# The first half of an encoder layer rebuilt: token-major inputs by chunks, 14 Strassen units, recurrence beside query/key, attention beside branch A

## The chip, the cores and the metric

One core of a Trainium2 chip runs one program. Its engines work side by side, each through its own list of instructions in order: PE (matmuls; PEld is the load of its stationary operand), DVE (vector), ACT (scalar), POOL (GpSimd) and SP, whose only work here is to issue transfers. Matmuls read SBUF and write PSUM, which has 8 banks of 128 x 512 fp32 here. The metric is the device time of one execution in microseconds (us); lower is better.

## The reference

One layer over 1024 tokens of width 1024: a gated linear recurrence (branch A), banded attention (branch B), their gated sum, a feed-forward block, and a gated embedding. Cut to what matters:

```
h = rmsnorm(x, norm_mix_g)
z = h @ w_in            # 5632 columns
qa, fa, ia, ga, qb, kb, vb, gate_a, gate_b = split(z)      # 7 x 512, 2 x 1024
oa = hgrn2_mixer(qa, fa, ia, ga, ...)    # 4 heads of 128: a recurrence over chunks with a decay per key
ob = band_attention(qb, kb, vb, ...)     # 8 heads of 64: each 64-token chunk sees itself and the 8 before
merged = sigmoid(gate_a) * (oa @ w_branch_a) + sigmoid(gate_b) * (ob @ w_branch_b)
x = x + merged @ w_out
h2 = rmsnorm(x, norm_ffn_g)
x = x + (silu(h2 @ w_ffn_gate) * (h2 @ w_ffn_up)) @ w_ffn_down
h3 = rmsnorm(x, norm_ple_g)
x = x + sigmoid(h3 @ w_ple_gate) * (p @ w_ple_proj)
```

## The kernel before, in words

Everything is fp32. The large products split each operand into a high part in a shortened fp32 form and the rest (`hi`, `lo`; names `wh`/`wl`, `whi`/`wlo` for weights, pairs of slots `s` for activations) and take three matmuls for one: high by high, high by low, low by high. ACT casts the high part, DVE or POOL subtracts to get the rest. Activations are kept feature-major, 8 tiles of 128 features x 1024 tokens, in 32 "slots" `s`; products go feature-major (`feature`: 512 tokens move past 128 features of weights) or token-major (`token`: 128 tokens are stationary, 256 or 512 feature columns of weights move).

In order of the program:

- `first_norm` loads x in 8 chunks of 512 KB, scales and splits each into `self.u`, and multiplies every chunk into four banks, which become q and f of head 0. The division by the norm is done when a bank is evicted (`self.r` by token, `self.rb` as rows), so products need not wait for it.
- `hgrn_in(0)`, the rest of head 0: the recurrence's i and g, token-major, 256 columns. `gate_sums` meanwhile makes the sums of activations that a Strassen product wants.
- `gate_units`: 7 units. One unit (`strassen`) makes 256 features of the two branch gates with 7 block products of 12 matmuls each where a plain product would take 8. `first_weights` makes a unit's operands from its raw weights (`gate_load`, two buffers of the pool `raw`), `quad_item` makes sums of weights that the output and down projections use much later, and the sigmoid of a gate is stored to DRAM.
- The recurrence: `hgrn_mix(h)` is woven with `hgrn_in(h + 1)` by `weave`, which compares the shares that two streams have done of a planned total; the fourth with `attn_v`, the values of attention. A head goes through 7 levels (m = 1 to 64): 8 small fp32 matmuls of kt by q on PE, then on DVE the products of q and of kt by the decay, which the next level's matmuls read, then a masked copy. Then 8 chunk steps, each of which reads `state` on PE and updates it on DVE.
- `attention`: 32 steps (4 pairs of heads x 8 token blocks), each with scores, row maximum, exponential, normalising, transposes, product by values. Filler from `feed` stands between: `attn_in`, the query/key products (token-major, 256 columns), then two plain gate chunks.
- `branches`: both branches' products times their gates; then `out_proj`, in `passes` of Strassen products, and the feed-forward block and the rest, which the change leaves alone.

The order on each engine is the order of the code (`order` ties each instruction of PE, SP and the ones given by `self.V`, `self.A`, `self.G` to the one before), and a tile's pool decides when a buffer comes free. All transfers but one small one are issued on SP, in order, and one that waits holds up those behind it.

## Time and profile before

| | |
|---|---|
| time of 3 runs | 1638.03 us median (1637.19 to 1640.42) |
| the profiled execution | 1640.24 us, of which the span from first to last instruction is 1638.5 us |
| granted clock of PE, mean | 0.991 |
| HBM read, written | 147.05 MB, 55.84 MB |
| transfers' share of the 16 DMA engines' span (queue q1) | 35.2% |

[...] The slices of the span show how evenly PE works and what clock it was granted:

```profile
PE   7999999999999999999898999999999999999998
DVE  8866666756649888665988788888888866536653
```

Each digit is the busy share of a fortieth of the span (41 us) in tenths. PE is at nine tenths or more but at the start and near the middle; DVE is busiest where attention runs (slices 12 to 16).

### The profile page before, as it was taken

Reading aid. Unit: us, or ns where it says so; the run is one execution under the profiler, and the core shown is the slowest. Engines: PE = TensorE matmul, PEld = TensorE weight load, DVE = VectorE, ACT = ScalarE, POOL = GpSimd, SP = SyncE. Lnnn points to the kernel's source line nnn. Section 1 sums busy time; section 2 is a strip of 40 time slices with the busy share of each in tenths; the row PEclk is TensorE's granted clock in tenths of the full one; section 3 lists DMA queues with packets and bytes.
Section 4 is the critical chain, followed back from the end, with each engine's and each line's share of the span. In section 5 each row is a group of like instructions: output and inputs, shape, how many; then the busy total and the mean of one; then the engine's idle time right before and its main releaser. Section 6 shows DMA issues by size and latency. Waiting matters only on the chain.

```text
span 1638.5 us, 22553 instructions
## 1 busy us (share of the span) xinstructions
PE 1590.3 (97%) x8656; PEld 1348.1 (82%) x8656; DVE 1191.1 (73%) x1838; ACT 618.3 (38%) x1080; POOL 702.1 (43%) x408
## 2 busy tenths in 40 slices
PE   7999999999999999999898999999999999999998
PEld 5877779899899999888686788888888888888887
DVE  8866666756649888665988788888888866536653
ACT  5523322122037777610365422222222234436321
POOL 2233342221143332114422587777666765546420
PEclk9999999999999999999999999999999999999999
DMA  5045550201020011178434323233222268555521
GB/s 186 27 134 193 202 204 16 102 27 52 27 76 16 29 43 45 47 301 291 174 129 180 128 97 110 97 109 117 97 97 97 79 248 305 208 195 185 194 77 52
DMA packets 70524, 204.36 MB, mean 125 GB/s; under 512 B 7952, under 2 KB 8720, under 8 KB 68496
## 3 DMA queue, kind: packets, MB, share of 16 engines
q1 hardware_dynamic: 70272, 202.90, 35.2%
q8 instruction: 68, 1.11, 0.3%
q14 instruction: 40, 0.33, 0.1%
q10 hardware_dynamic: 144, 0.02, 0.0%
HBM read 147.05 MB, written 55.84 MB: 124 GB/s over the span
## 4 chain that ended last, share of the span: by engine, by line
PE 44%; DVE 6%; DMA 1%; ACT 1%; issue 1%; POOL 0%; SPq 0%; DVEq 0%; ACTq 0%
PE pm L81 44%; DVE s L52 5%; DMA wr<-in_sg 1%; DVE wl L124 1%; ACT s L52 1%; DMA wr<-in_su 0%; DMA wr<-d 0%; DVE q L52 0%; ACT whi L52 0%; DVE pl L52 0%; DVE wr L52 0%; ACT wh L121 0%; POOL s L854 0%; SPq L76 0%; ACT q L52 0%
## 5 line engine op out<-in xcount | busy, mean ns | idle before, releaser
L81 PE MATMUL pm<-s,wh 128*128 128x512 f32 (+1 forms) x1688 | 527.6, 394 | 14.7 <-DVE s L52 9.1
L81 PE MATMUL pm<-s,whi 128*128 128x512 f32 x1568 | 490.3, 394 | 9.5 <-DVE s L52 5.0
L124 POOL TENSOR_TENSOR wl<-wr,wh 128x1024 fp32r<-128x1024 f32 (+2 forms) x100 | 250.0, 2506 | 367.0 <-ACT wh L121 356.0
L81 PEld LDWEIGHTS pm<-s,wh 128*128 128x128 f32 x1688 | 317.9, 190 | 82.7 <-DVE s L52 11.6
L81 PEld LDWEIGHTS pm<-s,whi 128*128 128x128 f32 x1568 | 295.2, 188 | 77.5 <-issue 3.1
L81 PE MATMUL pm<-s,wl 128*128 128x512 f32 (+1 forms) x844 | 330.6, 392 | 0.0
L81 PE MATMUL pm<-s,wlo 128*128 128x512 f32 x784 | 308.3, 393 | 0.3 <-DVE wlo L52 0.3
L52 DVE TENSOR_TENSOR s<-s,s 128x512 f32<-128x512 f32 (+3 forms) x202 | 252.6, 1277 | 74.2 <-ACT s L52 39.4
L81 PE MATMUL pm<-wh,s 128*128 128x256 f32 (+1 forms) x1152 | 252.1, 304 | 0.1
L121 ACT CAST wh<-wr 128x1024 fp32r<-128x1024 f32 (+2 forms) x106 | 106.3, 1005 | 286.5 <-PE pm L81 141.9
L52 POOL TENSOR_TENSOR wlo<-wr,whi 128x512 fp32r<-128x512 f32 x74 | 139.7, 1894 | 136.1 <-ACT whi L52 120.1
L81 PEld LDWEIGHTS pm<-wh,s 128*128 128x128 f32 x1152 | 191.4, 192 | 5.5 <-DVE s L52 0.3
L81 PEld LDWEIGHTS pm<-s,wl 128*128 128x128 f32 x844 | 160.7, 190 | 33.3 <-POOL wl L124 0.3
L81 PEld LDWEIGHTS pm<-s,wlo 128*128 128x128 f32 x784 | 147.8, 189 | 34.3 <-DVE wlo L52 0.7
L81 PE MATMUL pm<-wl,s 128*128 128x256 f32 (+1 forms) x576 | 170.5, 296 | 0.0
L52 DVE TENSOR_TENSOR t<-pm,t 128x512 f32<-128x512 f32 x143 | 98.1, 686 | 76.4 <-PE pm L81 71.2
L52 POOL TENSOR_TENSOR s<-s,t 128x512 f32<-128x512 f32 x44 | 75.4, 1713 | 90.0 <-ACT t L52 90.0
L81 PEld LDWEIGHTS pm<-wl,s 128*128 128x128 f32 x576 | 111.0, 193 | 2.1
L52 DVE TENSOR_TENSOR s<-pm,s 128x512 f32<-128x512 f32 x101 | 65.3, 683 | 60.6 <-PE pm L81 60.6
L52 ACT CAST whi<-q 128x512 fp32r<-128x512 f32 (+1 forms) x63 | 47.8, 758 | 155.2 <-DVE q L52 133.0
L81 PE MATMUL pm<-s,s 128*128 128x64 f32 (+4 forms) x776 | 99.2, 269 | 3.1 <-DVE s L52 2.9
L52 ACT CAST whi<-wr 128x512 fp32r<-128x512 f32 x90 | 67.2, 757 | 86.1 <-DVE wr L52 49.7
(141 smaller groups left out, 1954.3 us busy)
## 6 DMA issues: line engine op xcount, KB each, us to landing
s<-d SPq DMA_DIRECT2D x65, 512.0 KB, 5.4
d<-s SPq DMA_DIRECT2D x87, 256.0 KB, 2.7
d<-dq SPq DMA_DIRECT2D x60, 256.0 KB, 2.3
wr<-d SPq DMA_DIRECT2D x28, 512.0 KB, 3.6
dq<-in_wq SPq DMA_DIRECT2D x11, 1024.0 KB, 7.7
wr<-in_sg SPq DMA_DIRECT2D x22, 512.0 KB, 3.9
wr<-in_su SPq DMA_DIRECT2D x22, 512.0 KB, 4.2
d<-t SPq DMA_DIRECT2D x34, 256.0 KB, 2.8
```

The source lines that it names most:

```text
L52: return lambda *a, **k: self.trunk.order(op(*a, **k), self.key)
L81: return self.order(self.nc.tensor.matmul(*a, **k))
L121: self.nc.scalar.copy(hi[:, c], raw[:, c])
L124: rest.tensor_tensor(lo[:, c], raw[:, c], f32(hi[:, c]), ALU.subtract)
```

## The change

Everything up to the output projection is put in a new order; the feed-forward block and what follows stay.

- **First products.** Attention's values v (all 512 columns, 8 banks) are multiplied chunk by chunk as x arrives, the recurrence's i likewise in `second_rows`; both go to DRAM (`vd`, `id`) and are read back by head.
- **28 chunks in 14 units.** q, f, g of the recurrence and both branch gates (`CHUNKS`) are all made by Strassen units; q, f, g go to DRAM too and come back by `head_load`. A unit's raw weights are loaded alternately into the pool and into slots.
- **Recurrence.** The heads run one after the other (`heads`) with the query/key products as their filler (`attn_in`, now 512 columns, two token blocks at a time; scaled rows are stored to DRAM twice over, in pieces of 64, and loaded block by block). Some work moves from DVE to ACT: kt, the sums of squares, the scaling before the transposes.
- **Attention.** Keys of both heads of a pair lie side by side; the scores' sign is turned so that the minimum is taken; normalising moves from ACT and DVE to POOL; the transposes of both heads are copied four blocks at a time. The filler is what is left of query/key, then branch A's product (`branch_a`).
- **Branches and output projection.** Only branch B's products stay in `branches`; x is reloaded in two lots of four; the output projection's passes begin with the halves that are ready first (`OUT`).

```diff
-GATES = 7
+GATES = 14
+CHUNKS = [(n, h) for h in range(4) for n in "qf"] + [("g", h) for h in range(4)] + [(n, c) for n in "ab" for c in range(8)]
...
-        outs = [self.mm() for _ in range(4)]
+        outs = [self.mm() for _ in range(8)]
         xs = []
-        start = [self.unit() for _ in range(2)]
-        ws = [(hi, lo) for hi, lo, _, _ in start]
+        unit = self.unit()
         for k in range(KC):
             x = self.slot()
             sc = self.cols[:, C_MIX + k:C_MIX + k + 1]
+            if k and k % 2 == 0:
+                unit = self.unit()
+                self.unit_piece(unit, 0, D)
...
+            if k < KC - 1:
+                for b in range(8):
+                    self.token_step(outs[b], unit, k, b)
...
+        self.weights(0, ahead=2)
+        for b in range(8):
+            self.token_step(outs[b], unit, KC - 1, b)
+            if b == 0:
+                self.A.copy(piece(0), outs[0])
+            if b == 2:
+                self.norm_sums()
+        self.rows_out(outs, piece, 1)
+        self.A.activation(piece(0), piece(0), AF.Copy, scale=self.r[:, 0:1])
+        self.keep_rows(self.vd, got)
+
+    def token_step(self, ps, unit, k, b):
+        hi, lo = unit[:2]
+        c = slice(k % 2 * HALF, k % 2 * HALF + HALF)
+        ah, al = [t[:, b * P:b * P + P] for t in self.u[k]]
+        self.mul(ps, ah, hi[:, c], start=k == 0, stop=False)
+        self.mul(ps, ah, lo[:, c], start=False, stop=False)
+        self.mul(ps, al, hi[:, c], start=False, stop=k == KC - 1)
...
+    def second_rows(self):
+
+        outs = [self.mm() for _ in range(8)]
+        sums = self.gate_sums()
+        first = None
         for k in range(KC):
-            for i in (0, 2, 1, 3):
-                ah, al, bh, bl = pairs[i][k]
-                self.mul(outs[i], ah, bh, start=k == 0, stop=False)
-                self.mul(outs[i], ah, bl, start=False, stop=False)
-                self.mul(outs[i], al, bh, start=False, stop=k == KC - 1)
-        return outs
-
+            if k % 2 == 0:
+                (unit,) = self.weights(1, ahead=2)
+            for b in range(8):
+                self.token_step(outs[b], unit, k, b)
+            next(sums, None)
+            if k == 2:
+                first = self.gate_first()
+            if k > 3:
+                next(first, None)
...
-            raw = self.rp.tile([P, D], F32, tag="raw", name=f"wr{self.n}")
+            raw = self.slot() if len(self.sorder) % 2 else self.rp.tile([P, D], F32, tag="raw", name=f"wr{self.n}")
...
+                if kind == "g":
+                    s = self.stmp()
+                    A.activation(s, t, AF.Sigmoid)
+                    G.tensor_tensor(t, t, s, ALU.mult)
+                elif kind != "q":
+                    A.activation(t, t, AF.Sigmoid)
+                if kind == "f":
+                    G.tensor_scalar(t, t, self.lb1[:, i:i + 1], self.lb[:, i:i + 1], ALU.mult, ALU.add)
...
             def side():
-                more, item = iter(()), iter(())
+                more = iter(())
                 if n + 1 < GATES:
                     self.gate_load()
                     more = self.first_weights()
                 else:
-                    then()
+                    then(0)
                 flush()
-                if n:
-                    item = self.quad_item(1, 0)
-                    next(item)
-                yield
+                next(more, None)
+                for _ in range(2 if n else 0):
+                    next(item, None)
                 yield
                 next(more, None)
+                for _ in range(2 if n else 0):
+                    next(item, None)
+                yield
                 next(more, None)
...
+    def head_load(self, h):
+        q, f, v, g = self.hg[h] = [self.slot() for _ in range(4)]
+        self.load(f, self.gd[CHUNKS.index(("f", h))])
+        self.load(q, self.gd[CHUNKS.index(("q", h))])
+        self.rows_load(v, self.id, h)
+        self.load(g, self.gd[CHUNKS.index(("g", h))])
...
-        self.V.tensor_scalar(kt, f, -1.0, 1.0, ALU.mult, ALU.add)
+        nc.scalar.activation(kt, f, AF.Copy, scale=-1.0, bias=1.0)
...
-            yield 430 if m == 1 else 1560 if m < 32 else 1400 if m == 32 else 2000
+            yield 430 if m == 1 else 2400 if m < 32 else 1400 if m == 32 else 2000
...
-            yield 650
+            yield 450
...
+                for a in range(4):
+                    sl = slice(a * P, a * P + P)
+                    nc.scalar.activation(sq[:, sl], po[:, sl], AF.Square, accum_out=ss[:, a:a + 1])
...
+    def heads(self):
+        yield 10000
+        for h in range(4):
+            more = iter(())
+            if h < 3:
+                more = self.near(h + 1)
+            for i, ns in enumerate(self.hgrn_mix(h)):
+                yield ns
+                if i == 0 or i > 9:
+                    next(more, None)
...
+            to = self.qd[g, b] = self.spill()
+            for i in range(2):
+                self.store(
+                    to[:, :].rearrange("p (a two d) -> p a two d", two=2, d=64)[:, :, i, :], t[:, :].rearrange("p (a d) -> p a d", d=64))
+
+        for g in range(2):
+            ws = []
+            for two in range(0, 8, 2):
+                outs = [self.mm() for _ in range(2)]
+                for k in range(KC):
+                    if two == 0 and k % 2 == 0:
+                        ws += self.weights(1, ahead=3 - k // 2)
+                    for b in range(2):
+                        self.token_step(outs[b], ws[k // 2], k, two + b)
...
+        engine.tensor_scalar(s, s, den, None, ALU.mult)
...
+                self.attn_norm(sc[n, h][0], dens.pop((n, h)), self.G if n > 2 else self.V)
...
+            norm(n - 1, 1)
+            scores(n, 0)
...
+            if n + 5 < whole:
+                self.attn_load(*steps[n + 5])
+            exp(n, 0)
             drain(st)
+            scores(n, 1)
+            for _ in range(2 if n < 3 else 1):
+                next(feed, None)
+            pt(n - 1, 0)
...
             pt(n - 1, 1)
+            norm(n, 0)
+            pt(n - 1, 2)
+            exp(n, 1)
+            pv(n - 2)
...
+    def branch_a(self):
+        self.ma = []
+        while len(self.bsrc) < 4:
+            self.branch_src()
+        for dd in range(4):
+            (w,) = self.weights(1, ahead=0)
+            more = self.unit_pieces()
+            next(more)
+            for i in range(2):
+                t = self.slot()
+                self.load(t, self.gd[CHUNKS.index(("a", 2 * dd + i))])
+                self.ma.append(t)
+                for half in range(2):
+                    hs = slice(half * HALF, half * HALF + HALF)
+                    ps = yield from self.feature(w, self.bsrc, half, off=i * HALF, piece=1)
+                    next(more, None)
+                    self.V.tensor_tensor(t[:, hs], ps, t[:, hs], ALU.mult)
+                    yield 2592
...
+        other = [self.split(o) for o in self.ob]
...
+            if dd in (1, 2):
+                for _ in range(4):
                     x = self.slot()
-                    self.load(x, self.d["x"][c])
+                    self.load(x, self.d["x"][len(self.x)])
                     self.x.append(x)
...
+    OUT = [("A11", 0), ("S2", 0), ("A11", 1), ("S2", 1)] + [(w, i) for w in ("A12", "S3", "S1", "A22", "S4") for i in range(2)]
...
+                fill = self.attn_in()
+                weave(fill, self.heads(), 87000, 104000, whole=False)
+                self.attention(fill)```

Three places on PE show how the list of instructions moves. The first is the start of the program. In a row the left name is the PSUM bank (`pm`), then come the moving and the stationary operand, then the shape of the result; before, chunk 0 of x (its high and low part are `s_136` and `s_137`) moves past the stationary weights of two units:

```order
L81 MATMUL pm_125<-s_136,wh_130 128x512
L81 MATMUL pm_125<-s_137,wh_130 128x512
L81 MATMUL pm_125<-s_136,wl_129 128x512
L81 MATMUL pm_127<-s_136,wh_133 128x512
L81 MATMUL pm_127<-s_137,wh_133 128x512
L81 MATMUL pm_127<-s_136,wl_132 128x512
```

After, the weights of one unit move past 128-token pieces of chunk 0 (`s_141`, `s_142`):

```order
L82 MATMUL pm_129<-wh_138,s_141 128x512
L82 MATMUL pm_129<-wl_137,s_141 128x512
L82 MATMUL pm_129<-wh_138,s_142 128x512
L82 MATMUL pm_130<-wh_138,s_141 128x512
L82 MATMUL pm_130<-wl_137,s_141 128x512
L82 MATMUL pm_130<-wh_138,s_142 128x512
```

Before, a chunk of x feeds 4 banks with 12 matmuls; after, 8 banks with 24.

The second place is in a head of the recurrence, between two levels (`128x64 x8` are the 8 small matmuls of a level). Before, the end of one such stretch, with filler for the next head and four transposes of the head before:

```order
L81 MATMUL pm_2479<-s_170,wh_1990 128x512
L81 MATMUL pm_2479<-s_171,wh_1990 128x512
L81 MATMUL pm_2479<-s_170,wl_1989 128x512
L84 MATMUL pm_2489<-eye,m_2439 128x128 x4
L81 MATMUL pm_2495<-s_1789,s_2051 128x64 x8
```

It is preceded by 21 more dense matmuls since the level before. After, all of a stretch in head 0:

```order
L82 MATMUL pm_3105<-s_2922,s_3005 128x64 x8
L82 MATMUL pm_3128<-wh_2839,s_141 128x512
L82 MATMUL pm_3128<-wl_2838,s_141 128x512
L82 MATMUL pm_3128<-wh_2839,s_142 128x512
L82 MATMUL pm_3129<-wh_2839,s_141 128x512
L82 MATMUL pm_3129<-wl_2838,s_141 128x512
L82 MATMUL pm_3129<-wh_2839,s_142 128x512
L82 MATMUL pm_3136<-s_2922,s_3005 128x64 x8
```

The filler is now two blocks of query/key, 6 matmuls, and 12 in other stretches.

The third place is the end of attention (64x128 rows are products by values, `eye` rows transposes). Before, a gate product (24 matmuls, of which these are the first) follows the last products by values, and branch A's products follow it:

```order
L81 MATMUL pm_7391<-m_7340,s_3551 64x128
L81 MATMUL pm_7403<-s_136,wh_6150 128x512
L81 MATMUL pm_7403<-s_137,wh_6150 128x512
L81 MATMUL pm_7403<-s_136,wl_6149 128x512
L81 MATMUL pm_7403<-s_155,wh_6150 128x512
```

Branch B's operands were split under branch A. After, the last rows of attention and the first of branch B:

```order
L82 MATMUL pm_6557<-s_4595,wl_5082 128x512
L85 MATMUL pm_6669<-eye,m_6563 128x128 x4
L85 MATMUL pm_6675<-eye,m_6563 128x128
L85 MATMUL pm_6675<-eye,m_6585 128x128 x3
L85 MATMUL pm_6683<-eye,m_6585 128x128 x2
L82 MATMUL pm_6689<-m_6598,s_4519 64x128 x10
L85 MATMUL pm_6708<-eye,m_6640 128x128 x4
L85 MATMUL pm_6714<-eye,m_6640 128x128
L85 MATMUL pm_6714<-eye,m_6652 128x128 x3
L85 MATMUL pm_6720<-eye,m_6652 128x128 x2
L82 MATMUL pm_6724<-m_6668,s_4519 64x128 x10
L82 MATMUL pm_6736<-m_6707,s_4519 64x128 x10
```

The first row is the last of branch A's filler; the next row after these belongs to branch B, whose operands are split from the attention's output (`other`) only there.

More of the change, by code (lines that the diff above doesn't have):

```diff
@@ L124, in unit_piece, with unit_pieces @@
         rest.tensor_tensor(lo[:, c], raw[:, c], f32(hi[:, c]), ALU.subtract)
+    def unit_pieces(self):
+        hi, lo, raw, ap = self.unit()
+        self.load(raw, ap)
+        yield
+        for i in range(4):
+            c = slice(i * 256, i * 256 + 256)
+            self.nc.scalar.copy(hi[:, c], raw[:, c])
+            self.nc.gpsimd.tensor_tensor(lo[:, c], raw[:, c], f32(hi[:, c]), ALU.subtract)
+            if i == 3:
+                self.wready.append((hi, lo))
+            yield
     def weights(self, n=1, ahead=AHEAD):
@@ L666, in attn_stack, with attn_load @@
+        power()
+        self.scale = scale
+    def attn_load(self, pair, b):
+        qk = self.qk[pair, b] = self.small(HALF, tag="qk")
+        self.load(qk, self.qd[pair // 2, b][:, pair % 2 * HALF:pair % 2 * HALF + HALF])
     def attn_stack(self, pair, b):
@@ L749, in stack @@
             p, b = steps[n]
-            if b == 0:
-                for h in range(2):
-                    bt = self.small(640, tag="bias")
-                    self.load(bt, self.d["bias"][2 * p + h])
-                    self.bias[p, h] = bt
+            if b in (2, 5) and p < 3:
+                self.bias_load(p + 1, b == 5)
             return self.attn_stack(p, b)
         def scores(n, h):
-            stages = self.attn_scores(*steps[n], h)
-            sc[n, h] = (*next(stages), stages)
@@ L793, in attention @@
             pt(n - 1, 1)
-            next(feed, None)
-            stage(n, 0)
-            stage(n, 1)
-            pv(n - 2)
-            pt(n - 1, 0)
-            stage(n, 0)
-            yield 0
-        yield from feed
-    def gate(self, keep, late=False):
-        (w,) = self.weights()
-        t = self.slot(late=late)
-        keep.append(t)
-        for half in range(2):
-            ps = yield from self.feature(w, self.u, half, piece=2)
-            hs = slice(half * HALF, half * HALF + HALF)
-            self.nc.vector.tensor_tensor(t[:, hs], ps, self.rb[:, hs], ALU.mult)
-            yield 1296
+            norm(n, 0)
@@ new lines, in attention, with branch_src @@
+            pt(n - 1, 2)
+            exp(n, 1)
+            pv(n - 2)
+            if n >= whole - 2:
+                for _ in range(2 if n < whole else 0):
+                    t = self.slot()
+                    self.load(t, self.gd[CHUNKS.index(("b", len(self.gb)))])
+                    self.gb.append(t)
+            if n > 3 and self.scales:
+                self.scale()
+            next(feed, None)
+        drain(feed)
+    def branch_src(self):
+        o = self.oa[len(self.bsrc)]
+        hi, lo = self.slot(F32R), self.slot(F32R)
+        self.nc.scalar.copy(hi, o)
+        (self.nc.gpsimd if len(self.bsrc) < 2 else self.V).tensor_tensor(lo, o, f32(hi[:, :]), ALU.subtract)
+        self.bsrc.append((hi, lo))
```

514 lines of the change are left out of this document (236 added, 278 removed).

## The prediction

> **What bounds the kernel now.** I read the page first: the busy line says which engine could set the end.
>
> ```profile
> span 1638.5 us, 22553 instructions
> PE 1590.3 (97%) x8656; PEld 1348.1 (82%) x8656; DVE 1191.1 (73%) x1838; ACT 618.3 (38%) x1080; POOL 702.1 (43%) x408
> ```
>
> PE is busy 97% of the span, so time can only come from fewer PE microseconds or from PE's own waits. Next I cut PE's time into stages (view of windows: length, then busy us and count of each engine, granted clock, DMA share, GB/s).
>
> ```profile
> 5.00:34.19 29.19, 26.28 (x97) 20.23 (x98) 26.34 (x23) 19.75 (x22) 11.64 (x6) 0.94 0.58 224
> 34.19:66.67 32.48, 30.11 (x225) 29.71 (x224) 23.56 (x31) 13.49 (x23) 7.63 (x5) 0.89 0.05 17
> 66.67:213.00 146.33, 135.98 (x583) 108.62 (x582) 95.28 (x133) 50.02 (x82) 44.83 (x27) 1.00 0.51 174
> 213.00:240.00 27.00, 23.09 (x99) 18.49 (x98) 23.52 (x26) 6.91 (x9) 13.99 (x7) 0.87 0.43 149
> 240.00:474.00 234.00, 232.15 (x1680) 210.13 (x1680) 146.37 (x299) 44.86 (x78) 52.40 (x29) 1.00 0.14 49
> 474.00:660.00 186.00, 184.81 (x1671) 174.80 (x1670) 160.73 (x576) 135.89 (x390) 67.59 (x75) 1.00 0.13 43
> 660.00:690.00 30.00, 29.56 (x231) 24.39 (x229) 19.67 (x66) 17.29 (x41) 2.39 (x1) 1.00 0.01 1
> 783.90:806.00 22.10, 15.84 (x53) 11.99 (x53) 21.89 (x18) 9.02 (x10) 15.20 (x8) 0.85 0.46 170
> 925.00:1330.00 405.00, 403.20 (x1753) 329.25 (x1752) 342.36 (x319) 116.03 (x170) 305.76 (x173) 1.00 0.31 104
> ```
>
> They are: the first products; head 0's token products; the 7 Strassen units of gates; the start of the recurrence; recurrence; attention (two rows); start of the output projection; feed-forward. A matmul's duration in the groups is its latency, so I take the pace from start to start in the view in order of time: three 512-wide matmuls in 0.68 us (776.18 to 776.86), three 256-wide in 0.36 us (344.35 to 344.71).
>
> ```profile
> 344.35 0.40 PE L81 MATMUL pm<-wh,s 128*128 128x256 f32 x2
> 344.59 0.28 PE L81 MATMUL pm<-wl,s 128*128 128x256 f32 x1
> 344.71 0.40 PE L81 MATMUL pm<-wh,s 128*128 128x256 f32 x2
> 776.18 0.61 PE L81 MATMUL pm<-s,wh 128*128 128x512 f32 x2
> 776.64 0.39 PE L81 MATMUL pm<-s,wl 128*128 128x512 f32 x1
> 776.86 0.61 PE L81 MATMUL pm<-s,wh 128*128 128x512 f32 x2
> ```
>
> So a 512-wide matmul costs 0.227 us and a 256-wide one 0.120 us, 6% more per column. "Lost" below is a stage's length less its count at this pace.
>
> **The change part by part.** All against the profiled execution's 1640.2 us; the median of the runs shown is 2.2 us lower.
>
> *Streams.* Per 128 output features a plain product takes 48 matmuls of 512; a Strassen unit takes 84 for two. Removed: 10 feature chunks (480) and 1536 256-wide matmuls for the recurrence's token products and for query/key. Added: 7 more units (588), the recurrence's input i token-major (192), query/key 512 wide (384). Attention's own products keep their columns (192 calls in place of 208). Net 684 x 0.227 = +155.3 and 1536 x 0.120 = -184.3: **-29 us**. It is on the path: PE is the busy engine in each of these stages.
>
> *Start.* The first stage lost 29.2 - 97 x 0.227 = 7.2 us. The second has 192 256-wide matmuls, 23.0 us, and 33 small ones, some 4 us by the window's remainder, so it lost 5.5; its clock fell to 0.89 around the norm's sums. After, each 512 KB chunk of x feeds 24 matmuls (5.4 us) in place of 12, and the sums stand inside dense work. DVE's 26.3 us of that stage fit under 43.6 us of PE. I leave 5 us lost, for a cold start: **-8** (bounds -12 and 0).
>
> *Gate units.* 583 x 0.227 = 132.3 of 146.3 us: 14 lost in 7 units, 2.0 each. The feed-forward units, which have their raw weights one unit earlier, lost 405 - 1753 x 0.227 = 7.1 over 21 units, 0.34 each. PE's waits name the cause:
>
> ```profile
> PE pm L81 <- DVE s L52: 19.2, 13, 2.8
> PE pm L81 <- DVE t L52: 10.8, 7, 1.8
> PE pm L81 <- POOL m L484: 2.3, 2, 1.3
> ```
>
> One wait per unit is on a DVE sum (tile t), behind DVE work that starts late because raw weights share two buffers. The change alternates them with slots, so a unit's weights are asked for two units ahead. DVE's load per unit stays (95.3 of 146 us); POOL gets 16 small passes over f and g. I take 0.6 each, nearer to the feed-forward row: 8 lost, **-6** (bounds 5 and 28 lost: -9 and +14). SP gets a 256 KB store more for every half chunk; one is 0.33 us of its queue:
>
> ```profile
> 110.78 0.33 SPq L76 DMA_DIRECT2D d<-t  x1
> ```
>
> All stores and loads added come to some 40 MB; a unit then moves 4 MB in 20 us, 200 GB/s against 174 in the row above, under dense PE. I charge nothing; uncovered, it would delay a unit's weights, which are two units ahead.
>
> *Start of the recurrence.* 27 us hold 61 dense matmuls (13.9) and 38 small ones (about 5), 8 lost at clock 0.87. After, 42 dense matmuls (9.5 us) stand between the last unit and the first sums: **-5** (bounds -8 and 0).
>
> *Recurrence.* Here cover is removed. Four rows show a level and a state step:
>
> ```profile
> 226.79 3.47 DVE L52 TENSOR_TENSOR s<-s,s 128x512 f32<-128x512 f32 x2
> 238.83 1.89 PE L81 MATMUL pm<-s,s 128*128 128x64 f32 x16
> 240.53 0.70 PE L81 MATMUL pm<-s,wh 128*128 128x512 f32 x2
> 240.76 1.29 DVE L52 TENSOR_TENSOR s<-s,s 128x512 f32<-128x512 f32 x2 [3.35 <-PE pm L81]
> 472.01 0.39 PE L81 MATMUL pm<-state,s 128*128 128x128 f32 x2
> 472.81 0.34 DVE L52 SCALAR_TENSOR_TENSOR state<-state,s,pm 128x128 f32<-128x128 f32 x1
> 473.20 0.49 PE L81 MATMUL pm<-state,s 128*128 128x128 f32 x2
> ```
>
> After a level's matmuls end (240.53) DVE starts 0.23 us later and needs 1.29 us for the two products which the next level reads, 1.5 us in all; 3.47 us for them where POOL runs too. Before, 15 to 24 dense matmuls (3.4 us and more) or 24 narrow ones lie between levels; after, 6 or 12 of 512 (1.36 or 2.72). With 6, 0.2 us shows even undisturbed: 16 levels of 28, 3 us. POOL is busy 52 of 234 us; a quarter of the levels disturbed, 7, at about 1 us more on average over both covers (0.2 to 2.3): 7 us. Some 20 state steps of 28 stand without filler: from state product to state product takes 1.2 us at 472.01 with four transposes and one product between; I take 0.3 us uncovered: 6. Together 16; less the 2 us idle now, **+14**. Bounds: 0, if what DVE lost in evictions (one 512-wide pass in place of four 128-wide ones, kt and the squares' sums to ACT) removes the queueing; +70, if all 28 levels are disturbed. The new stores of query/key go out in 1024 pieces of 256 bytes; if issue time grew with pieces, 32 x 0.33 x 8 = 84 us of SP, an upper end, beside a 155 us stage in which SP only prefetches; the next head's loads are a head ahead.
>
> *Attention.* Filler falls from 24 narrow matmuls a step (2.88 us) to 6 wide ones (1.36); a full step is then about 5.4 us of PE. Engine work falls too: rows of a stretch in attention,
>
> ```profile
> L52 DVE TENSOR_TENSOR m<-pm,m 128x512 f32<-128x512 f32 x21 | 14.5, 692 | 0.7
> L52 DVE TENSOR_SCALAR m<-m,m 128x640 f32<-128x640 f32 x11 | 6.1, 555 | 0.4
> L52 ACT ACTIVATE m<-m,m 128x640 f32<-128x640 f32 x31 | 25.5, 824 | 9.3 <-DVE m L52 9.3
> L52 ACT ACTIVATE s<-pm,gq 128x128 fp32r<-128x128 f32 x42 | 15.5, 369 | 0.0
> L661 POOL TENSOR_SCALAR m<-m,m 128x4 f32<-128x4 f32 x21 | 6.3, 302 | 2.1
> L52 POOL TENSOR_TENSOR s<-s,t 128x512 f32<-128x512 f32 x44 | 75.4, 1713 | 90.0 <-ACT t L52 90.0
> ```
>
> DVE sheds the scaling of query/key (32 x 0.69), its square sums, half of the normalising and half of its 128-wide passes, some 70 of its 180 us in the two attention rows; ACT the other half of the normalising (16 x 0.82), its squares and half of its 128-wide copies, some 50 of 153. PE's own share there, from the groups of 474 to 690 us,
>
> ```profile
> L81 PE MATMUL pm<-wh,s 128*128 128x256 f32 x511 | 105.0, 291 | 0.0
> L81 PE MATMUL pm<-wl,s 128*128 128x256 f32 x255 | 71.9, 282 | 0.0
> L81 PE MATMUL pm<-s,wh 128*128 128x512 f32 x49 | 16.4, 413 | 0.0
> L81 PE MATMUL pm<-s,wl 128*128 128x512 f32 x24 | 9.5, 395 | 0.0
> ```
>
> is 216 - 766 x 0.120 - 73 x 0.227 = 107 us, and branch A adds 192 x 0.227 = 44: 151, against some 110 of DVE and 103 of ACT. PE stays ahead by more than before (216 against 180). The normalising goes to POOL, 640 wide, an operation that no row shows: over 0.30 us, and at the two-input row's rate 1.713 x 640/512 = 2.1 us. I take 1.6, nearer to the wide row; two a step, 3.2 of 5.4 us, so it hides. Pace **0** (bounds -8 and +25).
>
> The tail has no filler: the last two steps, then branch B waits for casts of the attention's output, which before stood under branch A.
>
> ```profile
> 777.60 1.05 ACT L52 CAST s<-s 128x1024 fp32r<-128x1024 f32 x1 [6.55 <-POOL s L854]
> 777.60 4.88 DVE L52 TENSOR_TENSOR s<-s,s 128x1024 f32<-128x1024 f32 x4 [3.53 <-POOL s L854]
> ```
>
> One cast and four rests of 1.2 us are 6 us, of which PE's own first products hide 2, plus 4 us of exponential, normalising and copies: **+8** (bounds 3 and 12).
>
> *Output projection.* 22.1 - 53 x 0.227 = 10 us lost, on sums that need branch B's last blocks. The new order asks first for operands that are ready after its half, and x is loaded in two lots: 3 stay, **-7** (bounds -10 and 0).
>
> The sum: -29 - 8 - 6 - 5 + 14 + 0 + 8 - 7 = -33, so 1607 against the profiled execution and 1605 against the median.
>
> [...]
>
> **Rivals.** (1) *The waits go altogether*: recurrence 0, gate units at 0.34 us, tail 4. That is 14 + 4 + 4 = 22 less: 1583. For it: DVE and ACT shed work in both stages. Against: cover is halved at the same places.
> (2) *Attention's chain shows*: maximum, exponential (0.82), POOL's normalising (up to 2.1), transposes, copy follow one another, with half the filler. One us in each of the 24 steps of three blocks or more: 1605 + 24 = 1629. Against: the normalised tile is used a step later.
> (3) *Slower: the recurrence loses its cover to POOL's contention.* Place: every level. Price: 0.23 + 3.47 - 1.36 = 2.3 us for 28 levels, 65 in place of 10: 1660. It is slower than before once the pair of products averages more than 2.7 us in place of 1.29, since (33 + 10)/28 = 1.5 us must come over the covered 1.36 - 0.23. Against: POOL works a quarter of that stage. For: waits there also cost clock; the row of 213 to 240 fell to 0.87 with no wait over 1.8 us.
> [...]
>
> **How the numbers follow.** Forecast 1605 (1593 to 1620) 0.45; rival 1 0.20; rival 2 0.20; rival 3 0.10; 0.05 spread over the rest. 8 in 10: down past rival 1 to 1575, up to 1641, past rival 2 and the gate units' upper bound, short of rival 3. About 0.2% (3.3 us) can be told from no change: faster 0.84, same 0.05, slower 0.11.
>
> **What would show it.** Changed profile: 512-wide matmuls 684 more, narrow ones gone; gate units near 19.7 us each; clock at 1.0 through the first norm; PE's waits on DVE in the recurrence near 0.2 us a level; a wait of about 5 us before branch B; almost none at the output projection. I am wrong if PE's busy share in the recurrence or in attention falls below 85%, or if a unit takes over 21 us.

## Result, and the profile after

The changed kernel is slower: 1653.22 us median (1650.36 to 1655.76) against 1637.61 for the kernel before, ratio 1.0093 with a 95% interval of 1.0071 to 1.0115. On another occasion the same pair gave 1.0060 (1.0043 to 1.0078), so a few tenths of a per cent between two comparisons mean little. The forecast was 1605. The profiled execution took 1655.76 us; its page begins:

```profile
span 1654.0 us, 21081 instructions
PE 1591.3 (96%) x7788; PEld 1303.0 (79%) x7788; DVE 1185.0 (72%) x1545; ACT 620.5 (38%) x1070; POOL 843.5 (51%) x492
PE   8999999999989989999999999999999999999998
PEclk9999999999889999999999999999999999999999
```

PE has 868 instructions fewer and is busy just as long: 1591.3 us against 1590.3. The work went and its time stayed. The windows of the stages show where (length, then busy us and count of PE, PEld, DVE, ACT and POOL, granted clock, DMA share, GB/s); they are the gate units, the recurrence, attention and the output projection:

```profile
98.60:383.30 284.70, 277.93 (x1178) 224.19 (x1177) 214.24 (x254) 86.54 (x143) 116.85 (x70) 0.98 0.56 198
383.30:579.20 195.90, 178.63 (x1089) 148.12 (x1088) 127.88 (x217) 53.84 (x151) 85.05 (x67) 0.91 0.36 110
579.20:754.20 175.00, 160.85 (x1243) 131.17 (x1241) 115.03 (x370) 118.29 (x302) 120.22 (x85) 0.99 0.38 122
798.50:882.30 83.80, 78.30 (x338) 64.06 (x337) 72.02 (x79) 46.15 (x56) 21.39 (x9) 0.98 0.39 131
```

Busy shares of 91 and 92% hide it: a PE at half clock is busy too (6.83 of the 6.83 us from 443.31 on, at clock 0.50). So each stage is measured by what it lost: its length less its matmuls at their quickest start-to-start pace (0.227 us for 512 columns, 0.12 for 256, 0.11 and 0.055 for most of the small ones), counted in the same way in both traces. The paces of the small ones move a stage's loss by some us, the same in both columns, so the change is firmer than the loss.

| stage | lost before | lost after | change | forecast |
|---|---|---|---|---|
| start | 13.7 | 2.9 | -10.8 | -8 |
| gate units | 14.5 | 18.0 | +3.5 | -6 |
| recurrence with its start | 19.0 | 48.2 | +29.2 | +9 |
| attention with its tail | 20.9 | 39.3 | +18.4 | +8 |
| branch products | 0 | 0.6 | +0.6 | 0 |
| output projection | 10.3 | 7.5 | -2.8 | -7 |
| feed-forward and the rest | 18.8 | 21.8 | +3.0 | 0 |

The changes add up to +41 where -4 was forecast; the streams fell by 26 where 29 was forecast. That is the whole miss of 48 us. The feed-forward block was not touched; its trace has three stretches of 3.4 us at half clock where the trace before has one. The recurrence's 48.2 consist of 22.1 in waits of over 0.3 us, 13.9 more of matmuls at half clock, and 12.1 in small gaps; before, these were 7.5, 2.9 and 8.5.

Two places in the view in order of time show the waits of the recurrence (start, length, engine, line, operation; in brackets the idle time before and what ended it). First a state step:

```profile
467.67 5.22 POOL L125 TENSOR_TENSOR wl<-wr,wh 128x1024 fp32r<-128x1024 f32 x2 [1.91 <-ACT wh L122]
468.23 2.37 DVE L53 TENSOR_TENSOR s<-s 128x8 f32<-128x8 f32 x1
471.13 2.92 DVE L53 TENSOR_TENSOR m<-s,s 128x512 f32<-128x512 f32 x2
473.97 0.28 DVE L53 COPY state<-pm 128x128 f32<-128x128 f32 x1
474.30 0.79 PE L82 MATMUL pm<-state,s 128*128 128x128 f32 x2 [2.05 <-DVE state L53]
```

A DVE pass over 8 columns takes 2.37 us while POOL works, and the next head's two products, which nobody needs yet, 2.92; the state's copy of 0.28 us stands behind both, and PE waits for it. Second, the start of a head:

```profile
485.43 1.01 POOL L627 TENSOR_TENSOR m<-m,mhalf 128x4 f32<-128x4 f32 x1
486.47 0.63 ACT L636 ACTIVATE m<-pm,m 128x128 f32<-128x128 f32 x2 [1.41 <-POOL m L627]
486.98 0.60 ACT L53 ACTIVATE m<-pm 128x512 f32<-128x512 f32 x1
487.61 0.69 DVE L53 TENSOR_REDUCE m<-m 128x8 f32<-128x512 f32 x1 [1.68 <-ACT m L53]
488.47 0.68 DVE L53 TENSOR_TENSOR s<-pm,eye 128x512 f32<-128x512 f32 x1
489.07 1.29 DVE L53 TENSOR_TENSOR s<-s,s 128x512 f32<-128x512 f32 x2
490.51 2.90 PE L82 MATMUL pm<-s,s 128*128 128x64 f32 x15 [3.84 <-DVE s L53]
```

PE waits 3.84 us for decay products that take 1.29. They stand on DVE behind the reduce of a query/key bank, which waits for ACT's square, which stands on ACT behind the last head's scaling, which waits for POOL's power. The granted clock fell after such waits. At the start of the head before, PE waited once, for 1.75 us. It was busy 1.66 of the 3.41 us from 439.90, still at full clock, and the next 6.83 us ran at half:

```profile
442.80 3.19 PE L82 MATMUL pm<-s,s 128*128 128x64 f32 x16 [1.75 <-DVE s L53]
439.90:443.31 3.41, 1.66 (x10) 1.13 (x9) 3.15 (x6) 1.14 (x4) 0.94 (x1) 1.00 0.01 4
443.31:450.14 6.83, 6.83 (x24) 5.88 (x23) 3.99 (x5) 0.00 (x0) 0.00 (x0) 0.50 0.00 0
```

### The profile page after: what moved, and what is told of

The parts are those of the page before. It is cut to its first block, busy times and chain, and to the rows that moved or that the text cites. A ratio compares the mean times of both kernels' runs of the same rounds, so it can differ in the third digit from the quotient of the medians.

```text
span 1654.0 us, 21081 instructions
## 1 busy us (share of the span) xinstructions
PE 1591.3 (96%) x7788; PEld 1303.0 (79%) x7788; DVE 1185.0 (72%) x1545; ACT 620.5 (38%) x1070; POOL 843.5 (51%) x492
## 4 chain that ended last, share of the span: by engine, by line
PE 41%; DVE 4%; DMA 3%; POOL 2%; issue 1%; ACT 1%; SPq 0%; DVEq 0%; ACTq 0%; POOLq 0%
PE pm L82 41%; DVE s L53 3%; DMA wr<-d 1%; POOL s L53 1%; DMA s<-d 1%; POOL wlo L53 1%; POOL wl L125 0%; DMA wr<-in_sg 0%; ACT s L53 0%; DMA wr<-in_su 0%; DMA wr<-in_dw 0%; SPq L77 0%; ACT whi L53 0%; DVE t L53 0%; DVE pl L53 0%
## 5 line engine op out<-in xcount | busy, mean ns | idle before, releaser
L82 PE MATMUL pm<-s,whi 128*128 128x512 f32 x1904 | 599.4, 396 | 3.2 <-DVE s L53 3.0
L82 PE MATMUL pm<-s,wh 128*128 128x512 f32 (+1 forms) x1368 | 425.1, 392 | 8.0 <-DVE s L53 7.8
L82 PEld LDWEIGHTS pm<-s,whi 128*128 128x128 f32 x1904 | 361.2, 190 | 86.9 <-issue 3.1
L82 PE MATMUL pm<-s,wlo 128*128 128x512 f32 x952 | 377.6, 397 | 3.0 <-POOL wlo L53 2.6
L53 DVE TENSOR_TENSOR s<-s,s 128x512 f32<-128x512 f32 (+3 forms) x225 | 266.9, 1211 | 76.3 <-ACT s L53 46.7
L125 POOL TENSOR_TENSOR wl<-wr,wh 128x1024 fp32r<-128x1024 f32 (+1 forms) x80 | 204.5, 2561 | 228.5 <-ACT wh L122 228.2
L82 PEld LDWEIGHTS pm<-s,wh 128*128 128x128 f32 x1368 | 253.1, 189 | 63.4 <-DVE s L53 9.5
L82 PE MATMUL pm<-s,wl 128*128 128x512 f32 (+1 forms) x684 | 265.8, 389 | 1.0 <-POOL wl L125 1.0
L82 PEld LDWEIGHTS pm<-s,wlo 128*128 128x128 f32 x952 | 180.7, 190 | 45.1 <-POOL wlo L53 3.0
L53 POOL TENSOR_TENSOR wlo<-wr,whi 128x512 fp32r<-128x512 f32 x74 | 143.8, 1954 | 103.3 <-ACT whi L53 98.9
L82 PE MATMUL pm<-wh,s 128*128 128x512 f32 x512 | 178.4, 415 | 5.3 <-ACT wh L122 5.3
L53 DVE TENSOR_TENSOR t<-pm,t 128x512 f32<-128x512 f32 x176 | 120.8, 686 | 82.8 <-PE pm L82 80.6
L122 ACT CAST wh<-wr 128x1024 fp32r<-128x1024 f32 (+1 forms) x87 | 87.3, 1007 | 182.3 <-PE pm L82 70.8
L82 PEld LDWEIGHTS pm<-s,wl 128*128 128x128 f32 x684 | 129.1, 189 | 27.6 <-POOL wl L125 1.4
L53 DVE TENSOR_TENSOR s<-pm,s 128x512 f32<-128x512 f32 x117 | 77.1, 685 | 74.4 <-PE pm L82 71.7
L53 POOL TENSOR_TENSOR s<-s,t 128x512 f32<-128x512 f32 x44 | 76.2, 1732 | 91.7 <-ACT t L53 91.7
L82 PEld LDWEIGHTS pm<-wh,s 128*128 128x128 f32 x512 | 101.4, 198 | 26.3 <-ACT wh L122 5.3
L53 POOL TENSOR_SCALAR m<-m,m 128x640 f32<-128x640 f32 (+4 forms) x58 | 90.6, 1573 | 46.0 <-DVE m L53 42.3
L53 ACT CAST whi<-q 128x512 fp32r<-128x512 f32 (+1 forms) x63 | 47.9, 760 | 157.4 <-DVE q L53 131.7
L82 PE MATMUL pm<-wl,s 128*128 128x512 f32 x256 | 104.1, 407 | 0.6 <-POOL wl L125 0.6
L53 DVE TENSOR_TENSOR dq<-dq 128x512 f32<-128x512 f32 x60 | 79.0, 1320 | 30.1 <-DMA dq<-in_wq 24.7
L53 ACT CAST s<-s 128x1024 fp32r<-128x1024 f32 x76 | 75.4, 1008 | 38.8 <-DMA s<-d 21.6
```

The source lines that it names most:

```text
L53: return lambda *a, **k: self.trunk.order(op(*a, **k), self.key)
L82: return self.order(self.nc.tensor.matmul(*a, **k))
L122: self.nc.scalar.copy(hi[:, c], raw[:, c])
L125: rest.tensor_tensor(lo[:, c], raw[:, c], f32(hi[:, c]), ALU.subtract)
```

## Experiments

All are variants of the changed kernel. Ratios are to the kernel before, run beside the variant; a time or a stage without an interval is that of one profile or one median.

**Control.**

> The changed kernel as it is, beside the variants of this call, so that differences of a few us are taken on one chip. 1648 to 1657.

The time was 1650.48 us, ratio 1.0060; the recurrence took 191.5 us, attention 174.1, the gate units 287.0. The recurrence of the same code thus differs by 4 us between two profiles, with the stretches at half clock (34 and 17 us). The variants widen this band: in the eight profiles whose recurrence is untouched it took 190.7 to 195.9 us, with 17 to 34 us at half clock; untouched, attention took 173.9 to 176.9 in ten, the gate units 281.5 to 287.3 in eleven. A difference inside such a band shows nothing.

**Twice the filler in the recurrence.**

```diff
-        self.mul(ps, ah, lo[:, c], start=False, stop=False)
+        for _ in range(1 + more):
+            self.mul(ps, ah, lo[:, c], start=False, stop=False)
```

`more` is 3 for the query/key pieces until attention begins, else 0, so the product with the low part is added four times.

> In the recurrence every piece of query/key filler is 12 matmuls of 512 instead of 6 (the product with the low part of the weights is made four times, so the query/key sums are wrong); 62 pieces lie in that stage, 372 matmuls more, 84 us at 0.227. Theory A (the filler is too thin to cover DVE's latency, and the waits it leaves also cost clock): most of the stage's 48 lost us go, so the stage grows from 196 us by 44 to 52 only, and the time from 1653 to about 1697 to 1705. Theory B (the loss is DVE slowed by POOL, or small matmuls that cost clock whatever lies around them): the loss stays and the whole 84 us show, 1730 to 1737.

The time was 1718.87 us, 1.0481 (1.0465 to 1.0497); the recurrence took 266.0 us, 70 more where the added matmuls alone take 84. Neither theory holds: the loss fell from 48 to 34 us. PE's waits on the state fell (5.4 to 2.2 us in the view of waits), but at two head starts it waited 4.9 and 3.9 us. Filler cannot cover a wait at a place where none of it lies.

**State products a step earlier.**

```diff
-                self.mul(o, q[:, cs], state, start=False, stop=True)
...
-                self.V.scalar_tensor_tensor(state, state, cur[:, c:c + 1], pk[:, :P], ALU.mult, ALU.add)
+                self.mul(o, q[:, cs], states[c - 1], start=False, stop=True)
+            if c < 5:
+                update(c + 2)
```

`update(i)` makes chunk i's product and updates one of three state tiles; 0 and 1 stand ahead of the steps.

> State products and DVE's state updates are issued one chunk step earlier, with three state tiles in turn; no work is added or removed. Theory A: PE's waits on the state (5.4 us) go, and the half-clock stretches that follow state steps with them: 8 to 12 us less in the recurrence, about 1643. Rival (the levels, not the state steps, carry the loss and the clock): 0 to 4 us less, 1649 to 1653.

The ratio was 1.0034 (1.0015 to 1.0053) and the recurrence took 191.0 us, inside the band of the untouched one. The waits of 1.4 and 2.0 us at 427 and 469 stayed, since the first state still stands behind the same DVE work.

**Squares and reduces spread out.**

```diff
-                    if k == 0 and late:
+                    if k < 2 and sums:
+                        squares()
+                    if k == 2 and late:
                         power()
...
-                    self.A.activation(sq, outs[b], AF.Square)
...
-                    late.append((g, two + b, outs[b], ss))
+                    sums.append((g, two + b, outs[b]))
```

`squares()` holds the lines taken out here: square, reduce, scaling and `late.append`.

> The squares of a finished query/key bank and DVE's reduce of them are issued one after each of the next two pieces of filler instead of both at the moment that the bank ends; the work is the same. Theory E (at the start of a head and at a state step PE waits for a DVE instruction that stands behind a reduce, which waits for ACT's square, which stands behind ACT's work on the last head; so a queue, not DVE's speed, makes the 4.0 and 2.0 us waits): those at 486 and 426 us shrink to under 1.5 us, the recurrence falls from 196 by 4 to 10 us. Rival (the level's own chain on DVE is simply too long for the filler): the waits stay within 1 us of what they were, recurrence 192 to 197.

The ratio was 1.0053 (1.0037 to 1.0069). The wait at the head start fell from 3.84 to 1.61 us and the one at 427 from 1.79 to 0.45, as the queue theory said:

```profile
484.02 0.69 DVE L53 TENSOR_TENSOR s<-pm,eye 128x512 f32<-128x512 f32 x1 [1.16 <-PE pm L82]
484.63 1.28 DVE L53 TENSOR_TENSOR s<-s,s 128x512 f32<-128x512 f32 x2
486.06 2.04 PE L82 MATMUL pm<-s,s 128*128 128x64 f32 x16 [1.61 <-DVE s L53]
```

But the stage did not gain the 4 to 10 us: it took 193.6, and other state steps now waited 2.8, 2.2, 1.6 and 1.5 us. The 1.6 us left at the head start is the bare chain on DVE, with no filler beside it.

**POOL's long passes to DVE.** The rests of the sums' operands and of the query/key weights are issued on DVE in place of `nc.gpsimd`.

> In the recurrence the rests of the sums' operands and of the query/key weights move from POOL to DVE, so that POOL runs only the small powers there. DVE gets 9 x 0.69 and 5 x 1.2 us more. Theory F (POOL's long passes stretch DVE's: 2.92 and 3.22 us for pairs that take 1.29 alone, 2.37 us for a pass of 8 columns): the waits of 2.2 us at 472 and at the junction (1.8) go, 5 to 10 us less, 1643 to 1648. Rival (queue E): DVE has 12 us more to do ahead of the chain, 0 to 6 us more.

The ratio was 1.0089 (1.0057 to 1.0121) and the recurrence took 196.6 us. The stretching is gone and the wait is not:

```profile
470.19 0.16 DVE L53 TENSOR_TENSOR s<-s 128x8 f32<-128x8 f32 x1
472.00 1.28 DVE L53 TENSOR_TENSOR m<-s,s 128x512 f32<-128x512 f32 x2
473.36 1.30 DVE L53 TENSOR_TENSOR m<-m,m 128x512 fp32r<-128x512 f32 x2
474.92 0.80 PE L82 MATMUL pm<-state,s 128*128 128x128 f32 x2 [2.29 <-DVE state L53]
```

0.16 us in place of 2.37 and 1.28 in place of 2.92 show that POOL did slow DVE here. But the rests of the sums' operands (1.30 here) now stand in DVE's own queue ahead of the state.

**Four moves at once**: state ahead, squares spread, `yield 430` after the first level raised to 2400, `yield 10000` ahead of the first head to 16000 (and the planned total that `weave` compares with from 104000 to 118000).

> Four moves in the recurrence at once, with the same work: state products one step earlier, the squares of a finished bank spread over the next pieces, filler between the first and the second level of a head (its share raised from 430 to 2400), and 6 us more filler ahead of the first sums. Theory E2 (some 22 us of waits over 0.3 us stand at head starts, state steps and the junction, where no filler lies between a DVE result and its reader; one move alone lets them pass to the next such place): together the waits fall to about 8 us and the half-clock time with them, recurrence 193 to 172 to 180 us, total 1632 to 1640. Rival (the filler is used up at other places and the waits pass to the levels): recurrence 188 to 196 us.

The ratio was 1.0036 (1.0019 to 1.0052) and the recurrence took 189.0 us, 2 below the band. That is the rival's range: waits of over 0.3 us came to 23.5 us, at other places than the control's 23.8, and the time at half clock was 17 us in both.

**Normalising in attention.** First as before the change (`None` stands for ACT), then with POOL for the first head only:

```diff
-                self.attn_norm(sc[n, h][0], dens.pop((n, h)), self.G if n > 2 else self.V)
+                self.attn_norm(sc[n, h][0], dens.pop((n, h)), self.V if h else None)
+                self.attn_norm(sc[n, h][0], dens.pop((n, h)), self.G if n > 2 and h == 0 else self.V)
```

> Attention's normalising goes back from POOL to ACT (first head) and DVE (second head) as before the change. Theory C (transposes wait for POOL's 1.57 us passes and for the weight rests queued between them): attention gets 10 to 20 us shorter, 1633 to 1643. Rival (the chain from scores to transposes is too long for the thin filler whichever engine normalises): the waits pass to ACT and DVE, within 4 us of 1653.

> In attention POOL normalises the first head only, DVE the second (0.56 us in place of 1.57 for five blocks, on the head whose transposes follow soonest). Theory G (the loop exponential, normalising, transposes, copy, next exponential is longer than a step because of POOL): PE's 8.5 us of waits on POOL fall below 4 and attention from 175 to 163 to 170 us. Rival (DVE's maxima and copies are then late in its queue): attention 173 to 180.

With ACT and DVE the ratio was 1.0060 (1.0040 to 1.0079), and attention took 181.1 us, 6 more: theory C falls, PE then waits for DVE and ACT (11.1 and 5.4 us in all). With POOL and DVE it was 0.9998 (0.9982 to 1.0015), and attention took 165.9 us, 8 less than the control and in theory G's range. (The 1.57 us of both expectations is POOL's mean over all widths; the pass over five blocks took 1.94.) The groups of the changed kernel in that stage (busy us, mean ns) and PE's waits there (us in total, times, longest):

```profile
L53 POOL TENSOR_SCALAR m<-m,m 128x640 f32<-128x640 f32 x32 | 61.7, 1939 | 25.2 <-DVE m L53 21.5 <-PE pm L82 3.7
```

```profile
PE pm L85 <- POOL m L53: 8.5, 10, 1.8
```

The same views with the second head on DVE, and the stage's window:

```profile
L53 DVE TENSOR_SCALAR m<-m,m 128x640 f32<-128x640 f32 x16 | 10.3, 644 | 0.6
```

```profile
PE pm L85 <- POOL m L53: 3.4, 3, 1.6
```

```profile
580.50:746.40 165.90, 157.43 (x1241) 131.35 (x1241) 128.76 (x399) 117.46 (x302) 78.39 (x56) 0.99 0.40 128
```

So it was not POOL as such: the first head's passes stayed there, and on ACT they did worse. Harm came from the second head's pass. Whether its place just ahead of its transposes did it, or two passes of 1.94 us in one step, these runs don't separate. PE's waits in the stage fell from 13.3 to 8.3 us in the view of waits; what is left of the loss, some 9 us more than before the change, stays open.

**The second head's exponential ahead of the copies**, with POOL and DVE as above: `norm(n, 0)` and then `exp(n, 1)` now stand between `pt(n - 1, 0)` and `pt(n - 1, 1)`.

> DVE normalises the second head as in the run before, and the second head's exponential is issued on ACT ahead of the copies of its predecessor's last transposes. Theory G2 (what is left of attention's loss is the same loop through ACT's order): attention 166 to 158 to 163 us. Rival (the copies then come late and PE waits for them or for banks): 165 to 172.

The ratio was 1.0013 (0.9997 to 1.0029) and attention took 164.1 us: 1.8 less than without it, short of the theory's range. This is inconclusive, and in the combined kernels below attention took 165.0 us without the move and 165.6 with it.

**Gate units.**

```diff
                 next(more, None)
+                next(item, None)
                 yield
                 flush()
                 next(more, None)
...
                 flush()
                 next(more, None)
-                next(item, None)
                 yield
```

The second run has this and g's multiply on DVE (`G.tensor_tensor(t, t, s, ALU.mult)` becomes `V.tensor_tensor`).

> The load of each quad item of the gate units is issued two products earlier, in the third slot of its unit instead of the last. Theory D (DVE's sum at the head of the next unit waits for this 1 MB load, and the unit's own sums queue behind it): the waits of 3.1, 1.9 and 2.2 us and their half-clock stretches go, gates 285 to about 275 us, 1643 to 1645. Rival (the unit's own raw weights come late): no change or later weights, 1651 to 1657.

> Gate units with the quad item's load two products earlier, and the multiply of a head's g by its sigmoid on DVE (8 passes of 512) in place of POOL. Theory H (what is left of the gate units' waits, 2.1 us at 210 and at 233, is DVE waiting for POOL's rests, which queue behind POOL's passes over g in units 5 and 6): gates 280 to 272 to 275 us. Rival (DVE now waits for ACT's sigmoid inside its own queue): gates 279 to 285.

With the load earlier the ratio was 1.0014 (1.0001 to 1.0026) and the gate units took 279.6 us; with g on DVE too, 1.0024 (1.0005 to 1.0042) and 278.9. Theory D has the mechanism: in the changed kernel DVE and PE waited as follows, and with the load earlier DVE waited no more on `in_wq`, only on PE, ACT and POOL. But the stage fell to 279.6 and not to 275: PE still had three waits on DVE sums, the longest of 2.0 us, and that sum stands behind a DVE pass that waits for POOL's rest.

```profile
DVE dq L53 <- DMA dq<-in_wq: 20.0, 9, 3.4
PE pm L82 <- DVE t L53: 6.8, 3, 3.0
```

The effect of g on DVE is too small to tell.

**Combined**: the four moves, the quad item, g, and the second head normalised on DVE; then the rests of query/key weights and of branch A's operands to DVE as well. The rests of the sums' operands, which stood ahead of the state in the run above, stay on POOL this time.

> All of it: the four moves of the recurrence, the quad item earlier and g on DVE, the second head normalised on DVE. If the parts add up: gates 274, recurrence 176, attention 166, so some 38 us less than the changed kernel, 1612 to 1622, below the kernel before. If the waits of one stage are passed on to the next, 1630 to 1640.

> The combined version of before, with the rests of query/key weights and of branch A's operands on DVE instead of POOL while the recurrence runs. Theory F2 (in the combined version the largest waits left, 3.7 us at 447 and 3.6 us at 523, are pairs of decay products that took 4.82 and 4.64 us in place of 1.3 because POOL ran two passes of 1024 beside them): these go, recurrence 189 to 178 to 184 us, total 1620 to 1626. Rival (DVE's own queue, 10 us longer, delays the same products): 187 to 193 us.

The times were 1630.58 us, 0.9931 (0.9905 to 0.9957), and 1625.43, 0.9915 (0.9887 to 0.9943). The recurrence took 188.7, then 182.8 us. So the parts did not add up in the first (176 was forecast for the recurrence), while the second came out in theory F2's ranges. In the first, two weight rests on POOL and a level beside them:

```profile
445.59 5.12 POOL L125 TENSOR_TENSOR wl<-wr,wh 128x1024 fp32r<-128x1024 f32 x2
446.44 4.82 DVE L53 TENSOR_TENSOR s<-s,s 128x512 f32<-128x512 f32 x2 [1.39 <-PE pm L82]
451.41 0.82 PE L82 MATMUL pm<-s,s 128*32 128x32 f32 x23 [3.55 <-DVE s L53]
```

In the second, at the same level, PE does not wait:

```profile
447.24 1.29 DVE L53 TENSOR_TENSOR s<-s,s 128x512 f32<-128x512 f32 x2 [1.39 <-PE pm L82]
448.45 1.22 DVE L125 TENSOR_TENSOR wl<-wr,wh 128x1024 fp32r<-128x1024 f32 x1
448.67 0.70 PE L82 MATMUL pm<-s,s 128*32 128x32 f32 x32
```

At this place the two products take 1.29 us in place of 4.82, and the wait of 3.55 us is gone. What that is worth as a whole is less sure: the stage fell by 6 us between two profiles, part of it clock (17 us at half clock, then 10), and the ratio by 0.0016, with intervals that overlap. Nor do the two trials compare the same move: alone it included the rests of the sums' operands, here it does not.

**Output projection.** `self.m_split()`, which casts an operand and takes its rest, is called twice, not once, inside branch B.

> The second operand of the output projection is cast and its rest taken inside branch B, as the first is, so that three operands stand ahead of DVE's sums of the second half instead of two. Theory I (the two waits of 2.3 and 3.6 us at the output projection are rests that queue on DVE behind those sums): both shrink to under 1 us, the stage falls from 83 to 77 to 80 us. Rival (DVE has the same work in the stage, and the wait goes to the next operand): 82 to 84 us.

The ratio was 1.0073 (1.0053 to 1.0093); the stage took 80.0 us in place of 83.8, the theory's upper end. In the thirteen profiles without this move it took 81.7 to 85.4, so the gain is 2 us or more. In the changed kernel its two waits ended with DVE passes that queue behind the sums:

```profile
806.45 0.50 PE L82 MATMUL pm<-s,wh 128*128 128x512 f32 x1 [2.10 <-DVE s L53]
808.58 6.96 DVE L53 TENSOR_TENSOR s<-s,s 128x1024 f32<-128x1024 f32 x4
815.59 0.79 PE L82 MATMUL pm<-s,wh 128*128 128x512 f32 x1 [3.40 <-DVE s L53]
```

Here one wait of 2.1 us was left.

**All together**, with a head's transposes one chunk step later (`if c == 6` to `c == 7`).

> Everything that helped together: the run before (recurrence mended, POOL's long passes off it, quad items earlier, second head normalised on DVE), the second operand of the output projection early, the second head's exponential ahead of the copies, and the transposes of a head's output one chunk step later (they waited 2.2 us at 510 for ACT's scaling). If the stages add up: output projection 3 to 5 us less, attention 1 to 2 less, recurrence 1 to 3 less, 1615 to 1621. If they collide: 1622 to 1630.

The time was 1618.93 us (1617.79 to 1619.35), 0.9870 (0.9848 to 0.9892): faster than both kernels. Against the run before, the output projection took 5.6 us less, the recurrence 2.3 less (less than profiles of the same code differ by) and attention no less. Its stages, in the order of the first table of windows:

```profile
99.40:378.30 278.90, 274.46 (x1177) 221.56 (x1177) 215.13 (x262) 86.64 (x143) 101.12 (x62) 0.99 0.58 201
378.30:558.70 180.40, 166.36 (x1090) 138.37 (x1089) 126.04 (x224) 52.64 (x151) 67.53 (x60) 0.97 0.39 122
558.70:724.30 165.60, 159.32 (x1240) 132.23 (x1240) 132.38 (x401) 117.96 (x302) 74.53 (x55) 0.98 0.39 127
768.70:848.50 79.80, 76.77 (x338) 62.82 (x337) 75.18 (x79) 44.29 (x54) 21.49 (x9) 1.00 0.41 129
```

The recurrence still loses 32.6 us, 16.4 of it in waits. The longest is again a head start. A weight rest that was moved to DVE waits there for ACT's cast, and the head's products stand behind it:

```profile
474.09 1.23 DVE L125 TENSOR_TENSOR wl<-wr,wh 128x1024 fp32r<-128x1024 f32 x1 [1.94 <-ACT wh L122]
475.96 1.28 DVE L53 TENSOR_TENSOR s<-s,s 128x512 f32<-128x512 f32 x2
477.39 0.88 PE L82 MATMUL pm<-s,s 128*128 128x64 f32 x3 [4.74 <-DVE s L53]
```

What would take these waits was not tried.

## Why the prediction was wrong

- **Streams** (-29) and **start** (-8) were right: -26 and -10.8. The sums of the norm cost no clock any more: it was 1.00 over the 98.6 us up to the gate units, where the stretch with the norm's sums had 0.89 before.
- **Recurrence** (+14, and -5 for its start) is the step that failed, by 20 us. It counted two kinds of places, levels and state steps, each as a bare DVE chain against the filler beside it. The state steps' total fits by luck (6 forecast; the six waits of over 0.3 us add up to 6.6): the price was 0.3 us at each of twenty, and two waits of some 2 us, at the first state of a head, make up most of it. The levels, the larger term with 10 us, had only some 0.6 in such waits; the 0.2 us at 16 levels would lie under that limit, and the small gaps did grow by 3.6. Two kinds of places were left out: the four head starts, where `yield 430` puts no filler between the sums and the second level (7.7 us in three of them), and the junction from the gate units to the first sums, which wait there for ACT's cast and POOL's rest of their operands (3.3 us, where a gain of 5 was forecast). And DVE's queue was not followed: squares' reduces and the next head's products stand ahead of what PE waits for.
- **The clock** was in the text as an argument for the third rival and had no term in the sum. It took 11 of the recurrence's 29 us in this profile (13.9 at half clock against 2.9). With 17 us at half clock in place of 34, the control can have lost 8.5 there at most.
- **Third rival** (POOL's contention, 0.10): DVE was slower beside POOL, at a few passes and not at every level: two pairs of the next head's products took 2.9 and 3.2 us, and two products of the levels 2.7 and 2.8; the mean of the 512-wide products was 0.77 us, below the 0.86 of before. Its total of 1660 was near for other reasons. Its point against, that POOL works a quarter of the stage, no longer held: 85 of 196 us after the change, 32 of them for the query/key powers and their scaling, which came into it.
- **Attention** (pace 0, tail +8): the normalising was sized at 1.6 us and measured 1.94, two a step. The rival of the visible chain was nearest to the mechanism and over-priced it: the stage lost 18 us more than before, where the forecast had 8 and that rival 32. Its point against, that the normalised tile is used a step later, holds for the first head only; the second is normalised (`norm(n - 1, 1)`) and transposed (`pt(n - 1, ...)`) in the same step. The tail was over-sized: it lost 4.0 us, and branch B began 0.2 us after the last product by values, for which a wait of 5 us was forecast.
- **Gate units** (-6): the change was +3.5. The raw weights were in time, and eleven units took 19.3 to 19.6 us, as forecast. Three took 23.0 to 24.3: the quad item, a load that the sum did not look at, was asked for just ahead of its first use.
- **Output projection** (-7): the change was -2.8. The order of operands was mended; the second operand's rest still queued behind the sums.
- Of the signs named for being wrong, the busy share did not show it: PE's stayed over 90% in both stages. The three long units did, at over 21 us, though the mean unit took 20.3. Lost time has to be taken from the pace, not from the busy share.

## What to carry to other kernels

Where filler is thinned, list every place at which a result of one engine is read by the next, head starts and junctions too, and ask at each what stands ahead of that result in its engine's queue; the result's own duration was often the smaller part of these waits (0.28 us in one of 2.05, 1.29 in one of 3.84). Work that is moved to another engine to free the first joins a queue there: POOL's rests on DVE ended one wait of 3.55 us and had a part in another of 4.74. Before a stage's length is read from one profile, measure how far profiles of the same code differ; here it was 5 us of 195, more than most single moves brought.

## What the hardware showed that was not expected

- The granted clock changed in fixed stretches. Between 60 and 1600 us of the profiles of the kernel before and of the changed kernel, each of the 18 times at half clock lasts 3.41 or 6.83 us, and within a trace they all begin on one raster of 3.41 us. They went with PE's busy share of the stretch before. Of the stretches at full clock, all 7 in which PE was busy less than 40% were followed by half clock, 10 of 17 between 40 and 60%, and 1 of 852 above. At 441 one wait of 1.75 us was enough. The longest wait ahead of each of the six times at half clock in the changed kernel's recurrence (34 us together) was 3.84 us once and 1.55 to 2.05 us at the other five.
- Whether a wait cost clock was then in part luck. The fourth head's start has the same wait of 1.61 us in both profiles of the changed kernel. In the first it lies within one stretch (PE busy 1.80 of 3.41 us) and 6.83 us at half clock follow; in the control it runs over into the next (2.01 and 3.22 of 3.41), and none follows.
- The stretching beside POOL was not in proportion to the DVE pass: 8 columns took 2.37 us beside POOL's weight rests and 0.16 without them, two products of 512 columns 4.82 us beside them and 1.29 without.
- POOL took 1.94 us to multiply 640 columns by a column, DVE 0.64.
